# A hybrid decoder block on one core: q and k projected four heads at a time, 512 columns per product, ahead of attention, and kept in DRAM

## The chip, the cores and the metric

The kernel runs on one core of one Trainium2 chip. The metric is the device time in microseconds (us), lower is better. The engines are named as the profile names them: PE is TensorE (matmul), PEld its weight load, DVE is VectorE, ACT is ScalarE, POOL is GpSimd, and SP is SyncE, whose queue issues nearly all DMAs of this kernel. PSUM is the memory that matmuls write; a PSUM bank here holds 128 x 512 numbers of 32 bits.

## The reference

One layer, batch 1, 1024 positions, width 1024, 8 heads. Each head has two queries and two keys of 64 numbers and one value of 128. Cut to what matters here:

```python
h = rms_norm(x, attn_norm_w)
q, k, v, u, g = split(h @ w_in)                  # 1024, 1024, 1024, 2048, 2048 columns
q = rms_norm(q.reshape(B, S, 8, 2, 64), q_norm_w)
k = rms_norm(k.reshape(B, S, 8, 2, 64), k_norm_w)
# per head, causal, with a relative-position bias:
p = softmax(q1 @ k1.T / 8 + bias) - lam * softmax(q2 @ k2.T / 8 + bias)
a = rms_norm(p @ v, subln_w) * (1 - lam_init)
y_a = a @ w_proj_attn
c = silu(layer_norm(causal_depthwise_conv(u_a * sigmoid(u_b))))   # 31 taps
y_b = c @ w_proj_conv
x = x + (sigmoid(g_a) * y_a + sigmoid(g_b) * y_b) @ w_out
x = x + (silu(gate) * up) @ w_down               # gate, up = rms_norm(x) @ w_gate_up
```

## The kernel before

Every product of two matrices is made of three matmuls (`mm3`, lines 152 to 155): each operand is split into a high part and a low remainder, and high x high, high x low and low x high are summed in PSUM. The split of a weight tile is a cast on ACT (line 120) and a subtraction on DVE (line 125).

The work has three stretches. In the first, `h` is made and turned into `hT` (columns in partitions), and then a list of items, `first`, is worked off by generators: `V` (half of v: 512 columns, kept in DRAM), `U` (128 columns of both halves of u for the convolution), `Q` (q and k of one head) and `G` (128 gate columns). At each step of a generator some convolution taps are released as well (`bg`, `TAPS_FIRST` per step): a tap is one DVE instruction over 128 x 1024 (line 610), 31 for each of eight channel blocks, the first of them line 604. The second stretch is attention: 64 steps, one for each head `h` and block `i` of 128 query rows. The third is the projections, the merge and the channel mixer.

An attention step `scores(h, i)` makes both score rows on PE (tile `sc`, three banks), adds the bias and takes the minimum of the negated scores on DVE (line 1153), the exponential and its sum on ACT (line 1158), and combines the two rows on DVE (lines 1164 to 1168). `turn` transposes the result on PE and splits it (ACT, then DVE); `weigh` multiplies it with v for two steps at once; `back` and `subln` finish a head. Between these, `more` puts products of the list `later` that do not depend on attention on PE ("fill"): q and k of the next head (`Q1` to `Q7`), and gates (`G0` to `G13`). The taps that are left are released in attention by `slack`, an estimate of how much longer PE takes for a step than DVE.

A `Q` item (`q_item`, line 790) loads the weights of one head by `ld_wide`: 128 columns of q and 128 of k side by side. `gemm_N` multiplies with `hT` as the stationary and the 256 weight columns as the moving operand; two blocks of 128 rows share one PSUM bank. ACT copies the bank (line 802) into the tile `qkraw` and sums squares for each group of 64 columns (line 805, eight instructions and eight reads of the accumulator a bank). DVE scales 512 rows by the norm (line 812). Later `turn_qk` transposes them on PE (tile `pQ`, line 821), ACT and DVE split them (lines 828 and 830), and DMAs of 128 KB on SP's queue move half rows into place (tiles `qs`, `ks`, `klo`).

The order of instructions on each engine is set when the kernel is built, by a scheduler that places them by its own estimate of times, within what the data and the code's `after(...)` demand; on the chip each engine then runs its own in that order.

Of the kernel before, what the change touches and what calls it, by code (L numbers as in the profile page):

```python
# [57 lines left out]
def kernel(  # L58
# [167 lines left out]
    neglam = cst.tile([P, 1], F32, name="neglam")  # L226
    lsum = cst.tile([P, 2], F32, name="lsum")
# [59 lines left out]
    def wraw():  # L287
        return wp.tile([P, 1024], F32, tag="wraw", name=nm("wraw"), bufs=2)
# [27 lines left out]
    def ld_wide(w, cols):  # L316


        def half(g):
            def go():  # L320
                raw = wraw()
                r3 = raw[:].rearrange("p (k c) -> p k c", c=256)
                o = 0
                for c0, n in cols:
                    nc.sync.dma_start(
                        r3[:, :, o : o + n],
                        w[512 * g : 512 * (g + 1), c0 : c0 + n].rearrange(
                            "(k p) c -> p k c", p=P
                        ),
                    )  # L330
                    o += n
                hi, lo = wsplit(raw)
                return (
                    hi[:].rearrange("p (k c) -> p k c", c=256),
                    lo[:].rearrange("p (k c) -> p k c", c=256),
                )

            return go

        return [half(0), half(1)]  # L340

# [30 lines left out]
    def kt(m, k):  # L372
        return m[k] if isinstance(m, dict) else m[:, k, :]
# [11 lines left out]
    def gemm_N(o, halves, shi, slo, i):  # L385

        ts = slice(i * P, (i + 1) * P)
        for k in range(NKT):
            whi, wlo = halves[k // 4]
            mm3(o, kt(shi, k)[:, ts], kt(slo, k)[:, ts], whi[:, k % 4, :], wlo[:, k % 4, :], k == 0, k == NKT - 1)  # L390


    v_hi = [dr.tile([S, 512], F32, name=f"v_hi{j}") for j in range(2)]
    v_lo = [dr.tile([S, 512], F32, name=f"v_lo{j}") for j in range(2)]
    a_d = [dr.tile([P, S], F32, name=f"a_d{h}") for h in range(H)]
# [15 lines left out]
    first = ["V0", "U0", "U1", "U2", "V1", "U3", "U4", "Q0", "U5", "U6", "U7"]  # L411
    later = [
        ["Q1", "G0", "G1"],
        ["Q2", "G2"],
        ["Q3", "G3"],
        ["G4", "Q4", "G5"],
        ["G6", "Q5"],
        ["Q6", "G7"],
        ["G8", "G9", "Q7"],
        ["G10", "G11", "G12", "G13"],  # L420
        ["G14", "G15"],
    ]
    TAPS_FIRST = 3.25
# [3 lines left out]

    def loads_of(it):
        c = int(it[1:])
        if it[0] == "V":  # L430
            return [ld_pair(win, k, V0 + 512 * c, tiles=vtiles) for k in range(0, NKT, 2)]
        if it[0] == "Q":
            return ld_wide(win, [(Q0 + c * P, P), (K0 + c * P, P)])
# [4 lines left out]
    for it in first[2:] + [x_ for l_ in later for x_ in l_]:  # L438
        ws.plan(loads_of(it))
# [203 lines left out]
    def g_half(c, sb, w, amid=None):  # L643
        o = gemm_T(w, hT_hi, hT_lo, sb, amid)
        sg = wp.tile([P, 512], F32, tag="sg", name=nm("sgg"), bufs=2)
        act.activation(sg[:], o[:], AF.Identity, bias=pcol("gate_b", c))  # L646
        nc.sync.dma_start(g_d[c][:, sb * 512 : (sb + 1) * 512], sg[:])
# [110 lines left out]

    def bias_rows():
# [18 lines left out]
    T = {}  # L778
    late = []

    pools = {}

    def qk_pool():

        if not pools:
            vw_ctx.close()
            pools["qk"] = qk_ctx.enter_context(tc.tile_pool(name="qkp", bufs=2, side="right", reuse_waits="tile"))
        return pools["qk"]

    def q_item(h):  # L790
        qkp = qk_pool()
        halves = [ws.next(), ws.next()]
        t = {}
        T[h] = t
        for b in range(2):
            raw = qkp.tile([P, 4, 256], F32, tag="qkraw", name=nm("qkraw"), bufs=2)
            ss = sm.tile([P, 16], F32, tag="ss16", name=nm("ss16"))
            for i2 in range(2):
                o = pg()
                for e in range(2):  # L800
                    gemm_N(o[:, 256 * e : 256 * (e + 1)], halves, hT_hi, hT_lo, 4 * b + 2 * i2 + e)
                act.copy(raw[:, 2 * i2 : 2 * i2 + 2, :], o[:].rearrange("p (e c) -> p e c", c=256))
                jk = sm.tile([P, VD], F32, tag="jk", name=nm("jk"), bufs=1)[:, :HD]
                for g in range(8):
                    act.activation(  # L805
                        jk, o[:, g * HD : (g + 1) * HD], AF.Square, accum_out=ss[:, 8 * i2 + g : 8 * i2 + g + 1]
                    )
                if i2 == 0:
                    yield
            r = rstd_of(ss[:], 16, 1.0 / HD, fast=h > 0)  # L810
            r4 = raw[:].rearrange("p i (g d) -> p (i g) d", d=HD)
            dve.tensor_tensor(r4, r4, r.unsqueeze(2).to_broadcast([P, 16, HD]), op=ALU.mult)

            def turn_qk(b=b, raw=raw):


                dma = nc.sync.dma_start
                for z, key in enumerate(("q", "k")):
                    pt = pm("pQ")
                    for i in range(4):  # L820
                        pe.transpose(pt[:, i * P : (i + 1) * P], raw[:, i, z * P : (z + 1) * P], ident[:])  # L821
                    w = pcol(key + "n")

                    def part(j):
                        return qkp.tile([P, 512], F32R, tag=f"{key}s{j}", name=f"{key}s{j}_{h}_{b}", bufs=2 if key == "q" else 3)

                    s1, s2 = part(1), part(2)
                    act.activation(s1[:], pt[:], AF.Identity, scale=w)
                    lo = part(3) if key == "q" else qkp.tile([P, 512], F32R, tag="klo", name=f"klo_{h}_{b}", bufs=1)
                    dve.scalar_tensor_tensor(lo[:], pt[:], w, f32(s1[:]), op0=ALU.mult, op1=ALU.subtract)  # L830
                    dma(f32(s2[HD:, :]), f32(s1[HD:, :]))
                    if key == "q":
                        lo2 = part(4)
                        for one, two in ((s1, s2), (lo, lo2)):
                            if one is lo:
                                dma(f32(two[HD:, :]), f32(one[HD:, :]))
                            dma(f32(two[:HD, :]), f32(one[HD:, :]))
                            dma(f32(one[HD:, :]), f32(one[:HD, :]))
                        t["q", b] = (s1, lo), (s2, lo2)
                    else:  # L840
                        dma(f32(s2[:HD, :]), f32(lo[HD:, :]))
                        dma(f32(s1[HD:, :]), f32(lo[:HD, :]))
                        t["k", b] = s1, s2

            late.append((NT * h if b and h else 0, turn_qk))
            yield

    inatt = [False]
    MAKE = {"V": v_item, "U": u_item, "Q": q_item, "G": g_item}

    def run(items):
        for it in items:
            gen = MAKE[it[0]](int(it[1:]))
            while True:
                n = len(late)
                if next(gen, gen) is gen:
                    break
                if not inatt[0]:
                    for _ in range(n):
                        late.pop(0)[1]()  # L860
                yield
# [225 lines left out]
    for _ in chain(opening(), run(first[2:])):  # L1087
# [15 lines left out]
    while late:  # L1103
        late.pop(0)[1]()
# [133 lines left out]
    inatt[0] = True  # L1238
# [3 lines left out]
    fill = run(it for l_ in later[:-1] for it in l_)  # L1242
    plan = [sum(4 if it[0] == "Q" else 2 for it in l_) for l_ in later]
# [15 lines left out]
    def slot(n, nq):  # L1259

        with after(last_fill[0]):
# [5 lines left out]
            for _ in range(nq):  # L1267
                if late[0][0] <= n:
                    late.pop(0)[1]()
# [7 lines left out]
    def slack_of(h, i):  # L1277

        p = (i + 1) * plan[h] // NT - i * plan[h] // NT
        nk = (i + 1) * P  # L1280
        t_pe = nk * (2.52e-3 + (2.5e-3 if i % 2 else 0.0)) + 5.15 * p
        t_dve = 0.4 + 4.2e-3 * nk + p + 0.3
        return max(0.0, t_pe - t_dve)
# [6 lines left out]
    for n, (h, i) in enumerate(steps):  # L1290
        if i == 0:
            load_bias(h)
        p = (i + 1) * plan[h] // NT - i * plan[h] // NT
        nq = len(late)
        scores(h, i)
        scm.append(last_mm[0])
        more((p + 1) // 2)
# [5 lines left out]
        more(p // 2)  # L1303
        slot(n, nq)
# [4 lines left out]
    assert next(fill, None) is None and not late  # L1309
# [61 lines left out]
    inatt[0] = False  # L1371
# [593 lines left out]
```

## Time and profile before

| | |
|---|---|
| median of 3 runs | 1739.37 us (1738.47 to 1739.49) |
| the profiled execution | 1738.13 us, span 1736.3 us |
| granted TensorE clock | 1.00 |
| busy, of the span | PE 1726.8 us, DVE 1292.2, ACT 794.8, POOL 27.1 |
| first score product | 312.3 us after the span's start |
| last score product | 805.8 us |

The page gives for each engine its busy time and, in its groups, line, engine, operation, output and input tiles, count, busy time, the mean duration of one, and idle time before them with what ended it. A "busy" PE does not mean that each matmul takes its recorded duration: the records of consecutive matmuls overlap.

### The profile page before, as it was taken

To read this page: it belongs to the slowest core of one execution; us is meant where nothing else is said; L and a number is where in the kernel's file an instruction comes from. 1 tells how busy PE (TensorE), PEld (TensorE's weight loads), DVE (VectorE), ACT (ScalarE), POOL (GpSimd) and SP (SyncE) were. 2 spreads that over 40 slices of the span, in tenths; PEclk is the share of its full clock that TensorE was granted. 3 is DMA by queue.
4 is the path that set the end of the run, shared out by engine and by line. 5 is a ranking of instruction groups with operands and counts; after the bars stand their busy time and mean duration, and the time that the engine had idled before them with its cause. 6 is when DMAs were issued, how large, how long until landed. Compare 5 with 4: busy or idle time off the path is not lost.

```text
span 1736.3 us, 25111 instructions
## 1 busy us (share of the span) xinstructions
PE 1726.8 (99%) x8954; PEld 1471.5 (85%) x8954; DVE 1292.2 (74%) x2202; ACT 794.8 (46%) x1873; POOL 27.1 (2%) x101
## 2 busy tenths in 40 slices
PE   9999999999999999999999999999999999999999
PEld 6878898999999998988888888888888888888887
DVE  8689988989889898885675567976676666565554
ACT  6121141667767776754564234633333333333332
POOL 0010000000000000000000000000000000000000
PEclk9999999999999999999999999999999999999999
DMA  7269545244444345364874677235445444697663
GB/s 244 91 201 305 183 124 136 71 120 131 122 142 114 89 120 151 87 173 139 288 245 134 200 246 251 86 107 178 152 159 172 158 149 152 224 352 241 218 216 131
DMA packets 260537, 295.22 MB, mean 170 GB/s; under 512 B 17730, under 2 KB 167283, under 8 KB 260412
## 3 DMA queue, kind: packets, MB, share of 16 engines
q1 hardware_dynamic: 257676, 283.73, 50.8%
q0 software_dynamic: 2432, 9.10, 2.2%
q8 instruction: 70, 1.15, 0.3%
q10 hardware_dynamic: 304, 0.79, 0.1%
q14 instruction: 55, 0.45, 0.1%
HBM read 189.19 MB, written 90.21 MB: 161 GB/s over the span
## 4 chain that ended last, share of the span: by engine, by line
PE 95%; DVE 2%; ACT 1%; DMA 1%; issue 0%; SPq 0%; DVEq 0%
PE acc L1819 22%; PE pg L153 14%; PE pg L154 14%; PE pg L155 14%; PE acc L532 12%; PE pg L737 4%; PE wo L1641 3%; PE sc L1152 2%; PE sc L1151 2%; PE pT L1187 2%; PE pW L155 1%; PE pW L153 1%; PE pW L154 1%; PE pQ L821 1%; DMA xa<-in_x_dram 0%; PE tr L1579 0%
## 5 line engine op out<-in xcount | busy, mean ns | idle before, releaser
L610 DVE SCALAR_TENSOR_TENSOR acc<-u,cw,acc 128x1024 f32<-128x1024 f32 x240 | 306.9, 1279 | 2.6
L153 PE MATMUL pg<-hT_hi,whi 128*128 128x512 f32 x512 | 201.5, 394 | 1.2 <-ACT sgg L646 0.9
L154 PE MATMUL pg<-hT_lo,whi 128*128 128x512 f32 x512 | 201.1, 393 | 0.0
L155 PE MATMUL pg<-hT_hi,wlo 128*128 128x512 f32 x512 | 200.8, 392 | 0.0
L120 ACT CAST whi<-wraw 128x1024 fp32r<-128x1024 f32 x101 | 106.3, 1052 | 149.0 <-PE pg L154 96.4
L125 DVE TENSOR_TENSOR wlo<-draw,whi 128x1024 fp32r<-128x1024 f32 x75 | 91.8, 1224 | 89.1 <-ACT whi L120 81.5
L125 DVE TENSOR_TENSOR wlo<-wraw,whi 128x1024 fp32r<-128x1024 f32 x102 | 124.3, 1219 | 44.7 <-ACT whi L120 41.4
L153 PE MATMUL pg<-whi,hT_hi 128*128 128x256 f32 x512 | 146.1, 285 | 0.3 <-ACT jk L805 0.3
L154 PE MATMUL pg<-wlo,hT_hi 128*128 128x256 f32 x512 | 145.7, 285 | 0.0
L155 PE MATMUL pg<-whi,hT_lo 128*128 128x256 f32 x512 | 145.3, 284 | 0.0
L120 ACT CAST whi<-draw 128x1024 fp32r<-128x1024 f32 x75 | 79.1, 1055 | 129.5 <-PE acc L532 119.3
L532 PE MATMUL acc<-wlo,whi 128*128 128x512 f32 x308 | 119.8, 389 | 0.0
L532 PE MATMUL acc<-whi,wlo 128*128 128x512 f32 x308 | 119.8, 389 | 0.0
L153 PEld LDWEIGHTS pg<-hT_hi,whi 128*128 128x128 f32 x512 | 96.2, 188 | 21.3 <-ACT sgg L646 1.7
L154 PEld LDWEIGHTS pg<-hT_lo,whi 128*128 128x128 f32 x512 | 96.2, 188 | 19.4 <-issue 0.6
L155 PEld LDWEIGHTS pg<-hT_hi,wlo 128*128 128x128 f32 x512 | 96.2, 188 | 19.2
L1158 ACT ACTIVATE E<-E,mn 128x256 f32<-128x256 f32 (+7 forms) x128 | 99.4, 778 | 28.2 <-DVE mn L1153 27.9
L153 PEld LDWEIGHTS pg<-whi,hT_hi 128*128 128x128 f32 x512 | 97.6, 191 | 1.9 <-ACT jk L805 0.5
L154 PEld LDWEIGHTS pg<-wlo,hT_hi 128*128 128x128 f32 x512 | 97.6, 191 | 1.5
L155 PEld LDWEIGHTS pg<-whi,hT_lo 128*128 128x128 f32 x512 | 97.6, 191 | 0.7
L1819 PE MATMUL acc<-h_hi,whi 128*128 128x512 f32 x240 | 93.4, 389 | 0.0
L1819 PE MATMUL acc<-h_lo,whi 128*128 128x512 f32 x240 | 93.4, 389 | 0.0
(321 smaller groups left out, 4182.2 us busy)
## 6 DMA issues: line engine op xcount, KB each, us to landing
wraw<-in_w_gate_up_dram SPq DMA_DIRECT2D x44, 512.0 KB, 4.6
wraw<-in_w_in_dram SPq DMA_DIRECT2D x37, 512.0 KB, 5.4
qs<-qs SPq DMA_DIRECT2D x96, 128.0 KB, 2.3
wd<-in_w_down_dram SPq DMA_DIRECT2D x44, 256.0 KB, 3.2
tdT<-wd SPq DMA_DIRECT2D x88, 128.0 KB, 4.2
draw<-sdS SPq DMA_DIRECT2D x44, 256.0 KB
draw<-tdT SPq DMA_DIRECT2D x44, 256.0 KB, 4.3
wraw<-in_w_in_dram SPq DMA_DIRECT2D x32, 256.0 KB, 4.6
```

The lines of the kernel that those rows point to most:

```text
L120: act.copy(dst, src)
L125: last_lo[0] = dve.tensor_tensor(dst, src, f32(hi), op=ALU.subtract).ins
L153: pe.matmul(o, lh, rh, start=start, stop=False)
L154: pe.matmul(o, lh, rl, start=False, stop=False)
L155: last_mm[0] = pe.matmul(o, ll, rh, start=False, stop=stop).ins
L532: m = pe.matmul(o[s_][i][:], l_[:, ts], r_[:, 512:], start=start and j + y_ == 0, stop=j == n - 1 and y_ == 2, skip_group_check=not start,)
L610: dve.scalar_tensor_tensor(acc[0][:], us[c][:, t : t + S], cw[:, c, t : t + 1], acc[0][:], op0=ALU.mult, op1=ALU.add)
L737: last_mm[0] = pe.matmul(o[:], l_, r_, start=first and n_ == 0, stop=last and n_ == len(terms) - 1).ins
L1151: pe.matmul(o[:, :w], qh[:, qs], k, start=True, stop=False)
L1158: act.activation(e[:, :nk], e[:, :nk], AF.Exp, bias=mn[:, j : j + 1], scale=-1.0, accum_out=l[:, j : j + 1])
L1641: last_mm[0] = pe.matmul(o[s_][i][:], l_, r_[:, k, :], start=start and g + k + y_ == 0, stop=g == 1 and k == 1 and y_ == 2, skip_group_che ...
L1819: pe.matmul(o[:], a_[x_][:, k, :], b_[y_][:, k, :], start=start and k + x_ + y_ == 0, stop=k == 3 and x_ == 1, skip_group_check=not start,)
```

## The change

The weights of q and k are no longer taken by head. Items `K0`, `Q0`, `K1`, `Q1` stand in the list `first`; each takes 512 columns (four heads) of k or of q, as the `V` items do, with the same weight tiles (`vwh`, `vwl`, four of each). A row block's bank now holds 128 rows x 512 columns of one of the two; ACT copies it and sums the squares into a table that is kept (`qkss`), and a DMA stores it in DRAM (`qk_d`). In attention, `qk_load` reads 512 rows of one head's q and k back from DRAM into `qkraw`, of which there is now one, `qk_norm` scales it, and `qk_turn` does what `turn_qk` did. `qk_turn` of a head stands three steps ahead of the head for its first half and one step into it for its second, and issues the next load. `later` is gates alone; their generator now yields after half of a 512-column sum, and one such half (12 matmuls) goes into every attention step except the first of a head. The last input item of the convolution, `U7`, stands last in the first stretch, and head 0 is prepared between its steps.

```diff
-    first = ["V0", "U0", "U1", "U2", "V1", "U3", "U4", "Q0", "U5", "U6", "U7"]
-    later = [
-        ["Q1", "G0", "G1"],
...
-        ["G14", "G15"],
-    ]
-    TAPS_FIRST = 3.25
+    first = ["V0", "U0", "U1", "V1", "U2", "K0", "U3", "Q0", "U4", "K1", "U5", "U6", "Q1", "U7"]
+    later = [f"G{c}" for c in range(2 * NKT)]
+    TAPS_FIRST = 3.0
...
     def g_item(c):
         w = ws.next()
         for sb in range(2):
-            g_half(c, sb, w)
+            cs = slice(sb * 512, (sb + 1) * 512)
+            o = pg()
+            for k in range(NKT):
+                mm3(o[:], w[0][:, k, :], w[1][:, k, :], hT_hi[:, k, cs], hT_lo[:, k, cs], k == 0, k == NKT - 1)
+                if k == NKT // 2 - 1:
+                    yield
+            g_out(c, cs, o)
             yield
...
+    def qk_item(z, j):
+        w = [ws.next() for k in range(4)]
+        for i in range(NT):
+            o = pg()
+            v_terms(o, TERMS, w, i, True, True)
+            raw = ap.tile([P, 512], F32, tag=f"v{'hl'[i % 2]}", name=nm("qkr"))
+            act.copy(raw[:], o[:])
+            jk = sm.tile([P, VD], F32, tag="jk", name=nm("jk"), bufs=1)[:, :HD]
+            for g in range(8):
+                act.activation(
+                    jk, o[:, g * HD : (g + 1) * HD], AF.Square, accum_out=qkss[:, i, "QK".index(z), 4 * j + g // 2, g % 2 : g % 2 + 1]
+                )
+            nc.sync.dma_start(qk_d[z][j][i * P : (i + 1) * P, :], raw[:])
+            yield
...
+    def qk_load(h, b):
+
+        raw = pools["qk"].tile([P, 4, 256], F32, tag="qkraw", name=nm("qkraw"), bufs=1)
+        for n_, z in enumerate("QK"):
+            nc.sync.dma_start(
+                raw[:, :, n_ * P : (n_ + 1) * P],
+                qk_d[z][h // 4][b * 512 : (b + 1) * 512, (h % 4) * P : (h % 4 + 1) * P].rearrange("(i p) c -> p i c", p=P),
+            )
+        QR[h, b] = raw
...
+        r4 = raw[:].rearrange("p i (g d) -> p (i g) d", d=HD)
+        dve.tensor_tensor(r4, r4, r.unsqueeze(2).to_broadcast([P, 16, HD]), op=ALU.mult)
...
+        if b == 0:
+            qk_load(h, 1)
+        elif h + 1 < H:
+            qk_load(h + 1, 0)
...
+    turns = {NT * h + d: (h, b) for h in range(H) for b, d in ((0, -3), (1, 1)) if h}
...
-        p = (i + 1) * plan[h] // NT - i * plan[h] // NT
+        p = int(i > 0)
...
-        more((p + 1) // 2)
+        more(int(i > 0))
...
-        slot(n, nq)
+        slot(n)
+        if n + 1 in turns:
+            qk_norm(*turns[n + 1])
```

In the built order, PE before: the last products of an input item of the convolution, then the first of `Q0`, 256 columns wide (the names are those of the tiles, a number telling one buffer from the next).

```order
L154 MATMUL pg_1934<-hT_lo,whi_1693 128x512
L155 MATMUL pg_1934<-hT_hi,wlo_1694 128x512
L153 MATMUL pg_1988<-whi_1832,hT_hi 128x256
L154 MATMUL pg_1988<-wlo_1833,hT_hi 128x256
L155 MATMUL pg_1988<-whi_1832,hT_lo 128x256
```

PE now: the same place in front of the first of the new items, `K0`.

```order
L154 MATMUL pg_1642<-hT_lo,whi_1224 128x512
L155 MATMUL pg_1642<-hT_hi,wlo_1225 128x512
L703 MATMUL pg_1707<-vwh_1528,hT_hi 128x512
L703 MATMUL pg_1707<-vwl_1529,hT_hi 128x512
L703 MATMUL pg_1707<-vwh_1528,hT_lo 128x512
```

1536 products of 256 columns are gone from the program, 768 of 512 are new, and of all of these only the transpositions are left in attention.

DVE in attention before: the scaling of `qkraw` (L812) stands among the splits of weights, the taps (L610) and the score minima (ISA, L1153).

```order
L125 TENSOR_TENSOR wlo_3369<-wraw_3365,whi_3368 128x1024
L610 SCALAR_TENSOR_TENSOR acc_2530<-u_1965,cw,acc_2530 128x1024
L812 TENSOR_TENSOR qkraw_2959<-qkraw_2959,r_3146 128x1024
L1153 ISA E_3275,mn_3263<-sc_3280,tb_2745,mn_3263 128x256
L1153 ISA mn_3263 128x1
L1168 RECIPROCAL rl_0_2761<-l_3264 128x1
```

DVE now, in the last step of head 5: the split of head 6's first half of k (`klo`, L807), and further down the scaling (L787) of its second half, which the loads put into the one `qkraw`; L568 is a tap.

```order
L807 SCALAR_TENSOR_TENSOR klo_0_7256<-pQ_7248,pvec,ks_6_0_7253 128x512
L568 SCALAR_TENSOR_TENSOR acc_5419<-u_3832,cw,acc_5419 128x1024
L1131 ISA E_7364,mn_7352<-sc_7365,tb_6796 128x512
L1131 ISA mn_7352 128x1
L125 TENSOR_TENSOR pl_7217<-pT_7311,ph_7216 128x4x128
L125 TENSOR_TENSOR pl_7217<-pT_7318,ph_7216 128x2x128
L1146 RECIPROCAL rl_5_6812<-l_7353 128x1
L787 TENSOR_TENSOR qkraw_7261<-qkraw_7261,r_7489 128x1024
L1131 ISA E_7364,mn_7352<-sc_7369,tb_6796,mn_7352 128x512
```

The scaling moved from among work that ScalarE had prepared to a place behind a load. In the whole order 112 taps of line 610 stood between the first and the last score minimum; 51 (now line 568) are left there.

SP's queue at the same place now: the two loads of that `qkraw` and the moves of half rows that stand around them.

```order
L814 DMA qs_6_0_7242<-qs_6_0_7239 64x512
L771 DMA qkraw_7261<-Q_d_119 128x4x128
L808 DMA ks_6_0_7254<-ks_6_0_7253 64x512
L815 DMA qs_6_0_7239<-qs_6_0_7239 64x512
L771 DMA qkraw_7261<-K_d_121 128x4x128
L818 DMA ks_6_0_7254<-klo_0_7256 64x512
```

Before, no load of q or k rows stood on this queue; the load of k's part now comes behind a move that needs ACT's split of k.

More of the change, by code (lines that the diff above doesn't have):

```diff
@@ L777 @@
     qk_ctx = ExitStack()
-    T = {}
-    late = []
+    T, QR = {}, {}
     pools = {}
     def qk_pool():
[L785 to L846, printed above, removed]
```

136 lines of the change are left out of this document (67 added, 69 removed).

## The prediction

> **What bounds the kernel now.** I read the page's busy times and chain first, then the busy times of three stretches: up to the first score product (312.3 us), attention (to the last score product, 805.8 us), and the rest.
>
> ```profile
> PE 1726.8 (99%) x8954; PEld 1471.5 (85%) x8954; DVE 1292.2 (74%) x2202; ACT 794.8 (46%) x1873; POOL 27.1 (2%) x101
> ...
> PE 95%; DVE 2%; ACT 1%; DMA 1%; issue 0%; SPq 0%; DVEq 0%
> ```
>
> ```profile
> 0.00:312.30 312.30, 309.55 (x1488) 254.19 (x1489) 262.54 (x310) 86.70 (x180) 11.87 (x32) 1.00 0.57 181
> 312.30:805.80 493.50, 492.17 (x3326) 451.48 (x3325) 435.67 (x1024) 337.25 (x1171) 15.05 (x68) 1.00 0.43 120
> 805.80:1736.30 930.50, 925.06 (x4143) 765.82 (x4142) 593.95 (x869) 370.84 (x522) 0.21 (x1) 1.00 0.58 193
> ```
>
> After the stretch and its length these list PE, weight load, VectorE (DVE), ScalarE (ACT) and POOL busy. TensorE (PE) is the bound everywhere, but in attention VectorE stands at 435.7 of 493.5 us, 88%. So attention's length can fall with its products only until VectorE binds, and that decides this case.
>
> A matmul's record reaches over the start of the next, so prices come from start to start. First a run of 512-column products, then one of 256-column products (start, duration), and the latter's group on the page:
>
> ```profile
> 51.11 0.39 PE L737 MATMUL pg<-vwh,hT_lo 128*128 128x512 f32 x1
> ...
> 61.76 0.39 PE L155 MATMUL pg<-hT_hi,wlo 128*128 128x512 f32 x1
> ```
>
> ```profile
> 218.59 0.28 PE L153 MATMUL pg<-whi,hT_hi 128*128 128x256 f32 x1
> ...
> 228.90 0.28 PE L155 MATMUL pg<-whi,hT_lo 128*128 128x256 f32 x1
> ```
>
> ```profile
> L153 PE MATMUL pg<-whi,hT_hi 128*128 128x256 f32 x512 | 146.1, 285 | 0.3 <-ACT jk L805 0.3
> ```
>
> 47 intervals in 10.65 us are 0.2266 us each; 86 in 10.31 us are 0.1199. The recorded durations (0.39 and 0.285) would promise 1536 x 0.285 - 768 x 0.39 = 138 us from the change; the starts do not.
>
> **PE, step by step.** All heads' q and k take 1536 products of 256 columns before, 768 of 512 after: 1536 x 0.1199 = 184.2 against 768 x 0.2266 = 174.0, a gain of 10.2 us. A sentence on a page: the Trainium skill, "TensorE: Matmul & The Clock Gate", section "Back-to-back issue gap", gives N/2.4 + 2.5 ns between starts, 109.2 and 215.8 ns here, by which widening would gain only 768 x 2.5 ns = 1.9 us, an estimate from that page; the trace shows 119.9 and 226.6, and I use those.
>
> By stretch, from the counts of the two orders. Before the first score there are 785 more 512-column products (1951 against 1166) and no longer 223 of 256: 312.3 + 177.9 - 26.7 = 463.5 us. In attention 1313 of 256 columns (157.4 us), 13 of 512 (2.9 us) and 18 weighted sums (2.2 us, moved behind) go: 493.5 - 162.5 = 331.0 us of PE. The rest is 930.5 + 2.2 - 0.9 = 931.8. With PE as the only bound the span would be 1726.3.
>
> So the first stretch costs 151.2 us more, the rest 1.3 more, and attention has to come down to 493.5 - 152.5 = **341.0 us to break even**.
>
> **VectorE in attention.** Its groups that shrink, and the one that stays:
>
> ```profile
> L610 DVE SCALAR_TENSOR_TENSOR acc<-u,cw,acc 128x1024 f32<-128x1024 f32 x113 | 144.2, 1276 | 0.0
> ...
> L125 DVE TENSOR_TENSOR wlo<-wraw,whi 128x1024 fp32r<-128x1024 f32 x27 | 32.9, 1219 | 2.2 <-ACT whi L120 2.2
> ...
> L812 DVE TENSOR_TENSOR qkraw<-qkraw,r 128x1024 f32<-128x1024 f32 x14 | 17.1, 1221 | 0.1
> ...
> L604 DVE TENSOR_SCALAR acc<-u,cw,pvec 128x1024 f32<-128x1024 f32 x3 | 2.5, 835 | 0.0
> ```
>
> More steps lie ahead of attention (80 against 52, at 3.0 taps instead of 3.25), so in the order 51 convolution taps are left in attention: 113 - 51 = 62 x 1.276 = 79.1 us go, two first taps 1.7, and 14 splits of q and k weights 14 x 1.219 = 17.1 (13 for gates stay). The scaling by the norm stays. That leaves 435.7 - 97.9 = **338 us**, more than PE's 331: VectorE becomes the bound, and its floor is within 3 us of break-even. Everything now hangs on how tightly it can be kept busy.
>
> What it waits for in attention today:
>
> ```profile
> DVE rl L1164 <- ACT E L1158: 14.1, 16, 2.0
> DVE E L1153 <- PE sc L1152: 12.1, 22, 1.7
> DVE rl L1168 <- ACT E L1158: 5.4, 13, 0.9
> DVE E L1153 <- PE pT L1187: 4.2, 6, 1.2
> ```
>
> These are links of one chain: score product, minimum on VectorE, exponential on ScalarE, combination on VectorE, transposition on PE. Its 58 us of waits (493.5 - 435.7) cost nothing while PE binds; once VectorE binds, each counts. How many remain no row shows. Bounds: none (338 us), or all (396 us). The fullest stretches, one ahead of attention (where independent taps fill), one inside:
>
> ```profile
> 160.00:200.00 40.00, 40.00 (x178) 33.11 (x177) 38.24 (x41) 4.96 (x7) 1.33 (x4) 1.00 0.58 194
> ...
> 400.00:440.00 40.00, 40.00 (x280) 37.07 (x280) 36.27 (x82) 26.84 (x78) 1.08 (x6) 1.00 0.39 109
> ```
>
> I take the upper, 38.24/40 = 95.6%, since a saturated engine always has a tap or split queued: 338/0.956 = 353.6 us.
>
> **The new wait: reloading q and k.** Before, the scaling (L812) read what ScalarE had copied from PSUM on the chip. Now the rows come from DRAM into a single buffer (qkraw, one buffer), free only when the preceding transpositions are done; the two loads stand on SP among the half-row moves of q and k, and the scaling (L787) holds VectorE's queue, behind it the score minima that PE waits on through three score banks. For one half head the order has these between the k split (klo) and the scaling: a tap (1.28), a minimum with its read (0.77), two splits (0.69, 0.42), a reciprocal (0.16), about 3 us of work. A load of that size and shape (256 KB in runs of 512 B), and its neighbours on the queue:
>
> ```profile
> qs<-qs SPq DMA_DIRECT2D x96, 128.0 KB, 2.3
> ...
> wraw<-in_w_in_dram SPq DMA_DIRECT2D x32, 256.0 KB, 4.6
> ...
> v_hi<-vh SPq DMA_DIRECT2D x16, 256.0 KB, 3.2
> ```
>
> 4.6 us to landing, issued near klo, leaves 1 to 3 us uncovered there. Over the 14 turns the work in between is 1.8 to 8.9 us, mean 4.6; against 4.5 us needed the shortfalls add up to 10 us, against 6 us (the k load behind more moves) to 22. I take 16. Bounds: 0, and 14 x 4.6 = 64. Attention: 353.6 + 16 = 369.6 us.
>
> **Edits costed at nothing, and their cover.** ScalarE gets the squares of q and k ahead of attention:
>
> ```profile
> L805 ACT ACTIVATE jk<-pg 128x64 f32<-128x64 f32 x224 | 50.7, 226 | 4.3
> L805 ACT ACTIVATION_READ_ACCUMULATOR jk<-pg 128x1 f32 x224 | 45.1, 201 | 0.0
> ...
> L802 ACT COPY qkraw<-pg 128x512 f32<-128x512 f32 x28 | 16.4, 586 | 18.2 <-PE pg L155 18.0
> ```
>
> Per block of rows 8 x 0.427 + 0.586 = 4.0 us, under that block's 24 x 0.2266 = 5.44 us of products; four PSUM banks cover an ACT delay, without them 32 blocks would each expose up to 4 us. Attention's ACT falls by about 110 us. The splits of the next wide weights wait on ScalarE for the previous wide item's last product; a convolution input item (96 products, 21.8 us) covers them, and v's second half does so today. The 32 stores of 256 KB to DRAM have 43.5 us per eight on a queue at 0.57 DMA share. Gate halves keep their products and stores. VectorE ahead of attention: 262.5 + 62 x 1.276 + 1.7 + 17.1 = 360 of 463.5 us.
>
> **The sum.** 463.5 + 369.6 + 931.8 = 1764.9 us of span. The profiled execution took 1738.13 us around its 1736.3; the median of the runs is 1.2 higher. 1764.9 + 1.8 + 1.2 = **1768 us**, 1.6% slower.
>
> **Rivals.**
> - *PE stays the bound.* Attention shrinks to PE's 331 us: 1726.3 + 3 = 1729, faster. For it: VectorE's floor is only 7 us higher, and my removed durations may be off by that; against: in-order VectorE at 100% is nowhere seen. It decides from an attention under 341 us.
> - *VectorE binds without waits.* 463.5 + 338 + 931.8 + 3 = 1736, no change to be told. For it: 51 taps are free to fill gaps; against: the 88% of today.
> - *The chain stays serial.* VectorE keeps its 58 us of waits and adds the 16: 338 + 74 = 412 us, 1810. For it: exponentials and minima alternate within one step; against: much of today's idling only waits for PE.
> - *The clock gate.* The trace's start shows PE at half pace after rest:
>
> ```profile
> 1.19 4.45 PE L929 MATMUL pg<-still 128*128 128x512 bf16 x10 [1.19 <-DVE still L166]
> 5.60 1.06 PE L929 MATMUL pg<-still,mark 128*128 128x512 bf16 x4
> ```
>
> Ten products in 4.45 us, then four in 1.06. If a wait in each head let the clock drop, each return would lose some 2.2 us, eight 18 us: 1786. Against: waits should be 1 to 3 us, with a gate half ahead. The Trainium skill, same page, section "Part 1: The HAM clock gate", says that an idle window of about 3.4 us halves the clock; the start agrees, and no wait in this trace tests it later (granted clock 1.00 throughout).
>
> **How the numbers follow.** Forecast 0.62 (alone 1750 to 1790: reload 0 to 40 us), PE bound 0.10, no waits 0.08, serial 0.13, clock 0.07. A measurement of this kernel tells about 0.2% from no change. Faster 0.10 and the same 0.08 are the first two rivals; slower is the rest, 0.82. A range from 1736 to 1800 leaves out the first rival and most of the serial one.
>
> **What would show it.** Right: first score near 463 us; attention near 370 with VectorE at 90% or more and PE idle some 39 us; the scaling (L787) waiting for qkraw's loads by about 16 us; the rest 932. Wrong: attention at 341 or less, PE without gaps there; a first stretch well over 464, from products waiting for wide weights or PSUM banks; a granted clock under 1.

## The result, and the profile after

The changed kernel takes **1845.82 us** (median of 6 runs, 1842.47 to 1856.15) against 1738.93 of before in the same runs (6 runs, 1738.12 to 1739.49): 1.0621 times, 95% interval 1.0594 to 1.0648. The forecast was 1768, with a range to 1800: the sign was right, the size was not, by 78 us. The profiled execution took 1847.99 us, with a span of 1846.1.

The page of the changed kernel, busy times, the granted clock in 40 slices, and the shares of the chain:

```profile
PE 1765.2 (96%) x8186; PEld 1455.8 (79%) x8186; DVE 1299.9 (70%) x2202; ACT 806.9 (44%) x1875; POOL 27.4 (1%) x101
...
PEclk9999999999989888898899999999999999999999
...
PE 84%; DMA 7%; DVE 5%; issue 2%; ACT 1%; SPq 1%; DVEq 0%; ACTq 0%
```

PE falls from 95% of the chain to 84%; DMAs, 1% before, are 7%, some 130 us. The three stretches (first score product at 463.9 us, last at 910.2), with the columns as before (the 805.8 us of before is the last score minimum; the last score product starts at 805.4, which changes nothing here):

```profile
0.00:463.90 463.90, 460.86 (x2051) 374.73 (x2052) 355.00 (x391) 186.80 (x676) 13.91 (x36) 1.00 0.50 161
463.90:910.20 446.30, 375.55 (x1978) 312.68 (x1978) 346.37 (x934) 247.24 (x672) 12.10 (x61) 0.91 0.44 127
910.20:1846.10 935.90, 928.74 (x4159) 768.42 (x4157) 598.57 (x880) 372.83 (x528) 1.38 (x4) 1.00 0.58 193
```

The forecast had 463.5, 369.6 and 931.8. Two stretches are right within 0.4 and 4.1 us; attention is 76.7 us too long. In it PE is idle for 446.3 - 375.6 = 70.8 us and VectorE for 99.9: neither binds. (PE's 375.6 are more than the 331 us of its products because the granted clock is 0.91 there: at the lower clock a record is longer.)

What PE's score products (tile `sc`) wait for in the changed kernel's attention: idle time in us, times, the longest:

```profile
PE sc L1129 <- DMA qs<-qs: 17.6, 6, 3.8
PE sc L1129 <- DMA ks<-klo: 10.1, 7, 4.1
PE sc L1129 <- DVE mn L1131: 7.4, 10, 1.8
...
PE sc L1130 <- DMA qs<-qs: 3.6, 4, 1.8
```

Three of these four are the half-row moves of q and k, 31.3 us (the weight loads in front of these products stand for much of the same time and are not added). Before, no score product waits for anything. The waits of VectorE in attention show the wait that the prediction was about, and a larger one above it, VectorE's share of the same late scores:

```profile
DVE E L1131 <- PE sc L1130: 28.8, 25, 5.2
DVE rl L1142 <- ACT E L1136: 13.3, 21, 1.3
DVE qkraw L787 <- DMA qkraw<-K_d: 13.2, 8, 3.5
```

One such place, head 1, in the chain that ends attention (start, us, what):

```profile
535.90 0.14 PE pW L155
...
536.06 0.12 ACT ar L1179
...
536.61 0.32 ACT qs L805
...
538.00 0.58 ACT ks L805
...
539.12 0.11 SPq L808
...
539.28 0.59 SPq L814
...
539.96 0.55 SPq L813
...
540.55 5.17 DMA qs<-qs
...
545.79 2.34 DMA qs<-qs
...
548.17 0.79 PE sc L1130
```

ScalarE's split of q (L805) comes behind a copy (`ar`) of the weighted sum on PE; the moves are issued from 538.6 us on, some only when an earlier one has landed (`one` is written over after it has been read twice), and the first score product of the fifth step stands for 3.8 us until moves have landed, a later one (548.17 us) until the last move of this chain has. From the first transposition of the turn (536.0 us) to the first score of the fifth step (546.7) it is 10.7 us; before, the same stretch took 9.1 to 19.2. What differs is what lies under it. Of the second halves' turns of heads 1 to 7 the stretch from the first transposition (tile `pQ`) to the first score of the fifth step, first and last head and the sum of the seven, of before:

```profile
385.30:397.00 11.70, 11.41 (x91) 10.61 (x90) 11.04 (x29) 11.38 (x58) 0.36 (x2) 1.00 0.56 138
...
751.70:770.90 19.20, 19.20 (x107) 16.53 (x106) 16.35 (x45) 10.98 (x35) 0.36 (x2) 1.00 0.64 172
sum 88.00, PE 87.59 PEld 82.04 DVE 74.42 ACT 65.01 POOL 2.65; mean PE 12.51 PEld 11.72 DVE 10.63 ACT 9.29 POOL 0.38
```

and of the changed kernel:

```profile
536.00:546.70 10.70, 4.09 (x23) 2.76 (x21) 9.22 (x28) 5.48 (x21) 0.79 (x4) 0.72 0.88 243
...
879.50:888.70 9.20, 5.89 (x34) 4.55 (x32) 5.48 (x13) 5.21 (x16) 0.36 (x2) 1.00 0.80 224
sum 72.70, PE 38.68 PEld 30.03 DVE 53.71 ACT 41.88 POOL 3.74; mean PE 5.53 PEld 4.29 DVE 7.67 ACT 5.98 POOL 0.53
```

Before, PE has 12.5 us of work under each turn and idles 0.4 us in all seven together. Now it has 5.5 and idles 34.0. The same stretches of the first halves (to the first step of the next head) add up to 95.5 us with 76.4 busy: 19.1 more. So 53 of the 70.8 us of idle PE lie under the turns.

The length of a step by its place in the head, from the starts of the score products, mean over eight heads (us from one step's first score to the next step's; the very last step ends at the last score product):

| step | 1 | 2 | 3 | 4 | 5 | 6 | 7 | 8 |
|---|---|---|---|---|---|---|---|---|
| before | 3.7 | 4.6 | 7.0 | 7.8 | 7.1 | 8.9 | 10.3 | 12.2 |
| after | 3.6 | 5.2 | 4.0 | **14.1** | **10.7** | 3.3 | 5.6 | 9.4 |

Steps 3 and 6 to 8, freed of fill, are now short; the fourth and fifth, where the second half is waited for, are 1.8 and 1.5 times as long.

### The profile page after: what moved, and what is told of

It reads as the page before. It is cut to its first block, busy times and chain, and to the rows that moved or that the text cites. A ratio compares the mean times of both kernels' runs of the same rounds, so it can differ in the third digit from the quotient of the medians.

```text
span 1846.1 us, 23765 instructions
## 1 busy us (share of the span) xinstructions
PE 1765.2 (96%) x8186; PEld 1455.8 (79%) x8186; DVE 1299.9 (70%) x2202; ACT 806.9 (44%) x1875; POOL 27.4 (1%) x101
## 4 chain that ended last, share of the span: by engine, by line
PE 84%; DMA 7%; DVE 5%; issue 2%; ACT 1%; SPq 1%; DVEq 0%; ACTq 0%
PE acc L1794 21%; PE pg L703 13%; PE acc L490 11%; PE pg L153 10%; PE pg L154 10%; PE pg L155 10%; DMA qs<-qs 2%; PE wo L1616 2%; PE sc L1129 1%; PE sc L1130 1%; PE pT L1165 1%; DVE E L1131 1%; DMA ks<-ks 1%; DMA ks<-klo 1%; PE pW L154 1%
## 5 line engine op out<-in xcount | busy, mean ns | idle before, releaser
L568 DVE SCALAR_TENSOR_TENSOR acc<-u,cw,acc 128x1024 f32<-128x1024 f32 x240 | 307.5, 1281 | 4.5
L153 PE MATMUL pg<-hT_hi,whi 128*128 128x512 f32 x512 | 206.4, 403 | 0.2 <-ACT hT_hi L120 0.2
L703 PE MATMUL pg<-vwh,hT_hi 128*128 128x512 f32 x384 | 148.8, 391 | 0.1
L703 PE MATMUL pg<-vwh,hT_lo 128*128 128x512 f32 x384 | 148.5, 390 | 0.0
L703 PE MATMUL pg<-vwl,hT_hi 128*128 128x512 f32 x384 | 147.9, 390 | 0.4 <-DVE vwl L125 0.4
L120 ACT CAST whi<-wraw 128x1024 fp32r<-128x1024 f32 x85 | 89.4, 1051 | 115.7 <-PE pg L154 67.6
L125 DVE TENSOR_TENSOR wlo<-wraw,whi 128x1024 fp32r<-128x1024 f32 x86 | 104.9, 1220 | 46.1 <-ACT whi L120 44.9
L1129 PE MATMUL sc<-ks,qs 128*128 128x512 f32 (+2 forms) x192 | 78.7, 415 | 47.0 <-DMA qs<-qs 17.6
L1131 DVE CUSTOM_DVE_ANT_0 E<-sc,tb 128x512 f32<-128x512 f32 (+3 forms) x128 | 74.2, 587 | 36.3 <-PE sc L1130 24.0
L1794 PE MATMUL acc<-h_hi,wlo 128*128 128x512 f32 x240 | 90.1, 389 | 0.0
```

The costliest lines, as they stand in the source:

```text
L120: act.copy(dst, src)
L125: last_lo[0] = dve.tensor_tensor(dst, src, f32(hi), op=ALU.subtract).ins
L153: pe.matmul(o, lh, rh, start=start, stop=False)
L568: dve.scalar_tensor_tensor(acc[0][:], us[c][:, t : t + S], cw[:, c, t : t + 1], acc[0][:], op0=ALU.mult, op1=ALU.add)
L703: last_mm[0] = pe.matmul(o[:], l_, r_, start=first and n_ == 0, stop=last and n_ == len(terms) - 1).ins
L1129: pe.matmul(o[:, :w], qh[:, qs], k, start=True, stop=False)
```

## The experiments

The theory: with the fill gone the steps became too short for a lead that is counted in steps, and the turns' half-row moves lie open. The rivals: VectorE's load, the clock gate, the reload, and SP's queue held by other work. "The time" is the median of a kernel's runs; attention is measured from the first to the last score product of the profiled execution.

**1. The turns two steps earlier** (e1)

```diff
-    turns = {... for b, d in ((0, -3), (1, 1)) if h}
+    turns = {... for b, d in ((0, -5), (1, -1)) if h}
```

> The turns of q and k stand two steps earlier: five steps ahead of a head for its first half, one step ahead of it for its second (before: three ahead, one into it). Theory 1 (the second half of q and k comes too late: reload, transposition, split and nine half-row moves do not fit into the three short steps before the fifth score step): the step before the fifth score falls from 10 to 18 us to about 6, attention from 446 us to about 375, the granted clock back to 0.99 or more, time about 1775 us. Theory 2 (VectorE is the bound, with 346 us of work and the waits of a serial chain): its work is the same, attention stays within 10 us of 446, time about 1840.

Measured: 1825.36 us, 1.0511 of before (1.049 to 1.0532); attention 421.2 us. The stretches under the second halves' turns are filled, their sum in this run:

```profile
sum 79.00, PE 79.00 PEld 68.57 DVE 60.10 ACT 49.23 POOL 0.07; mean PE 11.29 PEld 9.80 DVE 8.59 ACT 7.03 POOL 0.01
```

The fourth step falls from 14.1 to 6.8 us. But the seventh rises from 5.6 to 12.1, and only 20 us of the 107 are won. Where the turn now stands, the next link shows (chain of this run, head 1):

```profile
544.17 3.43 DMA qs<-qs
...
548.13 2.35 DMA qs<-qs
...
551.06 3.35 DMA qkraw<-K_d
...
554.43 0.04 DVE qkraw L787
```

The next reload stands on SP's queue behind the nine moves, the one buffer allows it no earlier, and the scaling (L787) holds VectorE (17.8 us in eight waits of this run, 13.2 in the changed kernel). Loads of v, 6.6 to 7.7 us each, stand in this run's chain in four heads as well. The time lies between those of the two theories: the place was right, and the next wait took over most of the gain.

**2. No half-row moves** (e2). Left out: the moves, and with them the second arrangement of q and k; the second score row reads the tiles of the first.

```diff
-            dma(f32(s2[HD:, :]), f32(s1[HD:, :]))
...
-                    dma(f32(two[:HD, :]), f32(one[HD:, :]))
-                    dma(f32(one[HD:, :]), f32(one[:HD, :]))
-                t["q", b] = (s1, lo), (s2, lo2)
+                t["q", b] = (s1, lo), (s1, lo)
...
-                t["k", b] = s1, s2
+                t["k", b] = s1, s1
```

> Leaves out the DMAs that move half rows of q and k (both score rows then use the same operand tiles, so the scores are others); everything else stays, the turns at their late places. Theory 1: the moves are most of the lead that is missing, so the long steps shrink and attention falls to about 380 us or less, time about 1780. Theory 2: no VectorE work goes, attention stays near 446, time about 1840.

Measured: 1783.59 us (one run). Its attention:

```profile
465.20:845.80 380.60, 349.56 (x1972) 292.32 (x1970) 335.79 (x925) 246.96 (x674) 11.87 (x61) 0.98 0.32 100
```

The moves are worth 446.3 - 380.6 = 65.7 us of attention. The waits for the reload go with them, since the reload no longer queues behind moves. PE's idle time falls by 39.7 us and its busy time by 26.0, with the granted clock at 0.98 instead of 0.91: a part of the 65.7 may be the slower products that the waits bring with them.

**3. Fewer taps in attention** (e3). Left out: all but two of the 31 taps of a channel block, from attention's start on, 41 VectorE instructions.

```diff
         def tap(t):
             def go():
+                if no_taps and t not in (4, CW - 1):
+                    return
...
+    no_taps.append(1)
     load_v(0)
```

> Leaves out nearly all of the 51 convolution taps that stand in attention (those that issue a DMA stay; the convolution of the last channels is then incomplete): 48 x 1.28 = 61 us less VectorE work there. Theory 2: attention falls by about 55 to 60 us, time about 1788. Theory 1: the long steps wait for DMAs, attention falls by less than 15 us, time above 1830.

Measured: 1824.98 us (one run), attention:

```profile
463.70:890.00 426.30, 371.11 (x1979) 311.42 (x1977) 304.06 (x893) 246.83 (x672) 11.98 (x61) 0.91 0.47 134
```

42 us less VectorE work give 20 us, which neither theory had (under 15, or as much as was taken out). So VectorE's work is a part of what sets the length, and not the whole. VectorE at 71% of attention still leaves it 426 us long: it is not the bound that the forecast took it for.

**4. Products that nobody reads, ahead of the fifth step's scores** (e4). Added: 36 products of 512 columns a head, 8 x 36 x 0.2266 = 65 us of PE work.

```diff
+        if i == NT // 2:
+            with after(scm[-1]):
+                o_ = pg()
+                for e in range(36):
+                    pe.matmul(o_[:], hT_hi[:, e % NKT, :P], hT_hi[:, e % NKT, 512:], start=True, stop=True)
         scores(h, i)
```

> Adds 36 products (8.2 us) whose result nobody reads ahead of the fifth score step of every head, 65 us of TensorE work in all. Theory 1: TensorE idles there anyway, the time stays within 15 us of the changed kernel's 1846. Theory 3 (a good part of the loss is the clock, at half for 85 us of the span, which costs up to 42 us): the idle stretches end, the granted clock goes to 0.99 and the time falls by 20 us or more. If TensorE had no idle time there, the time would grow by 65 us.

Measured: 1847.5 us (one run), attention:

```profile
463.80:911.60 447.80, 411.94 (x2267) 349.17 (x2266) 346.96 (x934) 249.46 (x674) 11.72 (x61) 0.98 0.45 127
```

The granted clock in attention rises from 0.91 to 0.98, 65 us of PE work were added, and attention is 1.5 us longer. PE's idle time falls from 70.8 to 35.9 us: much of the added work lies in time that was waited through. In sum the added work and the higher clock leave the time where it was, but the run doesn't show that the lower clock was free. By the starts of the score products, the fourth and fifth steps are 0.5 and 1.6 us a head shorter than in the changed kernel (13.6 and 9.1 us), and the sixth, behind the added products, is 3.1 longer (6.4). What the clock alone costs was not measured.

**5. Early turns and two buffers for the reload** (e5, the edit of e1 and):

```diff
-        raw = pools["qk"].tile(... tag="qkraw", ..., bufs=1)
+        raw = pools["qk"].tile(... tag="qkraw", ..., bufs=2)
...
-        if b == 0:
-            qk_load(h, 1)
-        elif h + 1 < H:
-            qk_load(h + 1, 0)
+        if h + 1 < H:
+            qk_load(h + 1, b)
...
+        qk_load(0, 1)
...
-            at = aps.tile([P, 512], F32, tag="at", name=nm("at"), bufs=2)
+            at = aps.tile([P, 512], F32, tag="at", name=nm("at"), bufs=1)
```

(`at` gives the room.)

> On top of the earlier turns (1825 us): two buffers for the reloaded rows of q and k, each load issued a whole turn ahead (room for it by one buffer less for the finished head's rows). Theory A (the reload comes late because its single buffer comes free late): VectorE's 18 us of waits for the reload go, with the chain behind them, time about 1800. Theory B (the nine half-row moves ahead of it on SP's queue hold it up): the loads now stand ahead of the moves, so the same 1800. Theory C (what is left are moves and v loads landing late, whatever the reload does): above 1815.

**6. Early turns, the reload on POOL's queue** (e6, the edit of e1 and, in `qk_load`):

```diff
-            nc.sync.dma_start(
+            pool.dma_start(
```

> On top of the earlier turns (1825 us), one buffer: the reloads of q and k are issued from POOL's queue, so that no move on SP's queue stands ahead of them. Theory B: the waits for the reload go, time about 1800. Theory A: the buffer comes free no earlier, the waits stay, time 1815 to 1830.

**7. The edit of e5, the reload and the loads of v on POOL's queue** (e8, `pool.dma_start` in `qk_load` and `load_v`)

> Earlier turns, two buffers for the reload, and both the reloads and the loads of v on POOL's queue, so that SP's queue holds only moves, weights, bias and stores. If the order on SP's queue is what is left (theory B, for v as well: 7 us to landing on the chain in four heads): about 1785. If the moves' own landing times are what is left: within 10 us of the kernel with two buffers.

Measured: e5 1812.46 us, 1.0421 of before (1.0391 to 1.0451), attention 411.7; e6 1817.47, 1.045 (1.042 to 1.048), 415.3; e8 1810.56, 1.041 (1.038 to 1.044), 408.8. The wait of VectorE for the reload is gone in e5, and it gives 9.5 us of attention beside e1; theories A and B had both asked for 1800 us, 12 less than measured. In e6 the waits fall to 8.9 us and do not go, so the single buffer and the queue both have a share. e8 is within 10 us of e5, so the order on SP's queue is not most of what is left. None brings more than 12.4 us of attention beside e1: each takes one link out and leaves the others.

**8. Before, without the moves** (e7; left out as in e2)

> The kernel before, leaving out the DMAs that move half rows of q and k. If the longer steps of its attention (7.7 us in the mean, against 5.6 to 7) hide them, its time stays at 1738 us within 4; the same edit gave the changed kernel 62 us. If they cost there too, it falls by 10 us or more.

Measured: 1736.73 us (one run), against 1739.38 for before in the same runs. The same moves that are worth 62 us in the changed kernel (1845.8 to 1783.6) are worth under 3 in the kernel before: the fill hid them.

**9. The gates twice** (e9). Added: each half of a gate sum is made twice, the second going into a PSUM bank that nobody reads or being written over.

```diff
+                if k % (NKT // 2) == 0:
+                    for e in range(NKT // 2 if k == 0 else 0):
+                        mm3(o[:], w[0][:, e, :], w[1][:, e, :], hT_hi[:, e, cs], hT_lo[:, e, cs], e == 0, e == NKT // 2 - 1)
+                    if k:
+                        d_ = pg()
+                        for e in range(NKT // 2):
+                            mm3(d_[:], w[0][:, e, :], w[1][:, e, :], hT_hi[:, e, cs], hT_lo[:, e, cs], e == 0, e == NKT // 2 - 1)
```

> The changed kernel, with the 12 products of every gate half in attention made twice: the first half's first go is overwritten, the second half's goes into a PSUM bank that nobody reads. That adds 56 x 12 = 672 products of 512 columns, 672 x 0.2266 = 152 us of PE work to attention (331 to 483 us), nothing to any other engine. Theory 1 (the turns' lead is counted in steps, and the steps became too short for the loads and moves; the added work fills the empty steps): attention ends near PE's own sum, 483 to 500 us, so 35 to 55 us more than the 446.3 of the changed kernel and not 152; the waits of scores for qs and ks nearly vanish; the granted clock is 1.00; the time is 1882 to 1902 us. Rival (the waits are a fixed length of time per head, whatever else PE does): attention 446 + 152 = 598 us, the time about 1998 us.

Measured: 1885.49 us (one run). Attention, and the sum of the stretches under the second halves' turns:

```profile
463.50:949.40 485.90, 482.58 (x2645) 412.60 (x2644) 353.70 (x943) 252.39 (x676) 12.56 (x62) 1.00 0.42 118
```

```profile
sum 77.90, PE 77.26 PEld 64.11 DVE 56.22 ACT 46.18 POOL 2.54; mean PE 11.04 PEld 9.16 DVE 8.03 ACT 6.60 POOL 0.36
```

152 us of work cost 39.6. PE is busy for all but 3.3 us, though the turns stand at the same steps of the code as in the changed kernel, and its score products wait for moves 3.3 us instead of 31.3: longer steps alone cover the moves. It also checks the floor: 482.6 - 152.3 is 330.3 us of PE's own work, against 331.0 in the prediction.

**10. Half wide** (e10): heads 0 to 3 as in the change, heads 4 to 7 by head in attention, with the edits of e5 and gates spread over the rest.

```diff
-    first = [... "K0", "U3", "Q0", "U4", "K1", "U5", "U6", "Q1", "U7"]
+    first = [... "K0", "U3", "Q0", "U4", "U5", "U6", "U7"]
+    for n_ in range(H * NT):
+        h_, i_ = n_ // NT, n_ % NT
+        own = {NT * q + d: f"H{q}" for q in range(4, H) for d in (-8, -7, -5, -4)}
+        fills.append([own[n_]] if n_ in own else ["G"] * (2 if h_ not in (3, 4, 5, 6) and i_ in (2, 5) else 1))
...
-        more(int(i > 0))
+        more(fills[n])
```

> A half of the change: q and k of heads 0 to 3 are projected 512 columns wide ahead of attention (K0 and Q0 alone), those of heads 4 to 7 as before by head, 256 columns wide, as fill in attention; gate halves are spread so that nearly every step has one item of fill; the turns lie at five steps and one step ahead of the head's first score (as in the earlier experiment with early turns), qkraw has two buffers. PE's own sum: first score at about 463.5 - 87 = 376.5 us, attention 331 + 4 x 192 x 0.1199 = 423 us, the rest 932. Theory 1 (fill in attention covers the loads, moves and the chain of score, minimum, exponential and combination): with 423 us of PE and about 390 of VectorE attention ends between 425 and 445 us, and the time is 1736 to 1758 us, near the kernel before and 70 us or more under the changed kernel with the early turns and two buffers (1812). Rival (the new path of q and k over DRAM is what costs, whatever the fill): its four heads over DRAM would keep half of that kernel's excess, some 30 to 40 us over PE's sum, and the time is 1765 to 1775 us.

Measured: 1759.83 us, 1.0121 of before (1.0104 to 1.0138). Attention:

```profile
379.90:827.50 447.60, 428.83 (x2732) 380.11 (x2730) 396.12 (x981) 295.03 (x950) 13.59 (x65) 0.99 0.45 128
```

2 us above what the first theory gave and 5 below the rival's: attention is 2.6 us over its upper end, and the first score 3.4 late. 86 us of the excess of 107 are gone, 33 of them with e5's edits alone (1845.8 to 1812.5) and 53 with four heads by head and the fill spread; four heads still go over DRAM, so that path is not by itself what costs. PE idles 18.8 us; its longest wait is for minima (8.4 us at nine scores). It does not beat the kernel before, and no run pointed to a version that would: by the intervals between products all eight heads could gain 10 us of PE, four heads half.

**11. Stores on another queue** (e11)

```diff
-        nc.sync.dma_start(g_d[c][:, cs], sg[:])
+        nc.scalar.dma_start(g_d[c][:, cs], sg[:])
...
-            nc.sync.dma_start(a_d[h][:, sb * 512 : (sb + 1) * 512], at[:])
+            nc.scalar.dma_start(a_d[h][:, sb * 512 : (sb + 1) * 512], at[:])
```

> The changed kernel, with the stores of gates (L604) and of attention's output (L1209) issued on ScalarE's own queue, behind the activation that makes their data, instead of on SP's queue. In the changed kernel's attention the SP queue stood 107.4 us (17 times) at the gate stores and 24.8 us (13 times) at the others, with half-row moves and loads of q, k and v behind them in order. Theory 1 (the second halves are turned too late for their nine moves, counted from the turn itself): the moves wait on one another and on their data, so the long steps stay (about 14 us the fourth of a head, 11 the fifth), attention falls by 15 us at most, and the time is 1831 to 1846 us. Rival (the moves are late because the queue in front of them is held): without the holds the fourth step of a head falls to some 7 us, attention by 40 us or more, and the time is 1805 us or less.

**12. The same on top of e5, with the first move on ScalarE's queue** (e12)

```diff
-            dma(f32(s2[HD:, :]), f32(s1[HD:, :]))
+            nc.scalar.dma_start(f32(s2[HD:, :]), f32(s1[HD:, :]))
```

> The earlier experiment with early turns and two qkraw buffers (1812 us), with the stores of gates and of attention's output and the first half-row move of each operand issued on ScalarE's own queue. There SP stood 70.9 us at the gate stores, 48.2 us at that first move (it waits for ScalarE's activation) and 29.9 us at the other stores. Theory 1 (what is left of the excess there is the chain of scores, minimum, exponential and combination, and the loads of v, none of it a held queue): the time stays within 10 us, 1802 to 1815 us. Rival (the held queue makes the loads of v, 5 to 8 us in the chain, and the moves late): attention falls from 411.7 to about 381, what it was with no moves at all, and the time is 1780 to 1785 us.

Measured: e11 **1856.19** us, 1.0679 (1.0663 to 1.0695), 10 us slower than the change itself, attention 454.1; e12 1803.79, 1.0378 (1.036 to 1.0395), attention 401.3. Taking the 132 us of holds off SP's queue brings the moves no nearer: the fourth and fifth steps of e11 still take 13.2 and 10.5 us, as the first theory had it, and SP now stands at the first move for 65.1 us (31.5 in the changed kernel) and at the loads of v for 52.8 (22.0). That e11 is slower neither theory had, and why was not followed up. In e12 the queue is worth some 9 us, within the first theory's range. The Trainium skill, "Perfetto Trace Analysis", section "DMA Optimizations", suggests one DMA-issuing engine for inputs and another for outputs; here that is 10 us worse in e11 and 9 better in e12, where a half-row move, no output, went along.

Attention's length against PE's own work in it, from these runs:

| | PE work, us (products x 0.2266 or 0.1199) | attention, us |
|---|---|---|
| changed | 331 | 446.3 |
| e4 | 331 + 65 = 396 | 447.8 |
| e10 | 331 + 92 = 423 | 447.6 |
| e9 | 331 + 152 = 483 | 485.9 |
| before | 492 (its busy time) | 493.5 |

With 331 and with 396 us of work attention is equally long; with 483 it is as long as PE's work. (e4 and e9 differ from the changed kernel by the added products alone. e10 has early turns and two buffers as well; with these edits and 331 us of work, e5 has 411.7 us, so 446 is no fixed length either.)

## Why the prediction was wrong

- **The first stretch and the rest**: 463.5 and 931.8 us forecast, 463.9 and 935.9 measured. The intervals of 0.2266 and 0.1199 us, the counts by stretch, and ScalarE's squares and the stores as hidden work all held. The Trainium skill's formula for the interval, which the prediction quotes beside its own, is by its section "Back-to-back issue gap" that of a product by itself and not of a stream; by its 109.2 and 215.8 ns the first stretch would have been 457.4 us, an estimate from that page. Of the 4 us in the rest no cause was sought.
- **PE's floor**: 331.0, checked by e9 at 330.3.
- **VectorE's work**: 338 forecast, 346.4 busy. The durations of VectorE's groups in attention, added up, fall by 99 us (502.7 to 403.4), about as forecast. But busy time counts records that overlap once, and it fell by 89.3. The prediction took recorded durations off a busy time, which it had avoided for PE.
- **"I take the upper, 38.24/40 = 95.6%"**: failed. Without the moves VectorE is at 335.8/380.6 = 88%, just what it was at before, and attention is 27.0 us longer than the 353.6 of this step. The fullest 40 us inside attention of before were not those that the prediction shows, but these, 94.7% full; such a share was reached for a while and not over the whole:

```profile
320.00:360.00 40.00, 40.00 (x254) 36.24 (x254) 37.86 (x77) 24.29 (x91) 0.75 (x4) 1.00 0.32 90
```

  e3 says why the share is no law: less VectorE work did not shorten attention by as much. With neither engine full, the chain of score, minimum, exponential and combination is the likely pace: e2's longest waits are its links (VectorE 18.0 us for exponentials, PE 11.2 for minima). No run isolates it.
- **"The new wait"**: 16 us forecast, 13.2 measured, eight waits of up to 3.5 us. The mechanism was right; it stands behind the moves on SP, as said. That the size came near is in part luck: the loads landed after 3.0 and 3.1 us (median), where the sum had 4.5 to 6, and eight turns of 14 waited.
- **"Edits costed at nothing, and their cover"** has no line on the turns, and this is the step that failed most. The change puts the second half's turn one step later than before, gives its nine moves a lead of a few *steps*, and also empties the steps. The prediction counted the 1313 products that leave attention as time won and didn't ask what they had covered: 10 us a turn, 14 turns. e2 prices it at 65.7 us, with the reload's 13.2 and the slower products in it; e7 shows that the moves cost under 3 us before, and e9 that fill covers them. 353.6 + 27.0 + 65.7 = 446.3, where the 27.0 is what is left over.
- **The rivals**: "the chain stays serial" gave 412 us by another cause (VectorE's 58 us of waits), and attention went past it. The clock gate came, at a granted clock of 0.91 in attention instead of 1.00. What it cost is not told apart: e4 mends most of the clock with 65 us of added work, and the time stays. "PE stays the bound" and "no waits" fell by 105 us and more.
- **Open**: e12 with all its mending stands 21 us over e2, which itself stands 50 over PE's floor. The waits there are many and of 1 to 3 us each; no run took them apart. Nor was the lower clock's own cost measured.

## What to carry to other kernels

A lead that is counted in loop steps is a time only as long as the steps keep their length: where a change takes fill out of a loop, list the transfers and turns that the fill covered, and multiply each one's latency by its count before anything is booked as won. In the built order, add up what an engine has to do between the issue of a transfer and its first reader; where that is 5 us and the latency 10, the rest is a wait. And when no engine is busy nearly throughout a stretch (here PE 84%, VectorE 78%), sums of busy time give a floor but no forecast: here a stretch took 446 to 448 us whether PE had 331 or 396 us of work in it.

## What the runs showed of the hardware

- The granted clock fell to 0.72 in a stretch of 10.7 us in which PE was busy for 4.1, and stayed at 1.00 in attention where PE was busy nearly throughout (e9). Around that stretch the changed kernel's rows (columns as before; the clock is the third number from the end) show when:

```profile
537.30:540.70 3.40, 1.35 (x8) 0.76 (x8) 3.30 (x6) 2.77 (x10) 0.00 (x0) 1.00 1.00 300
540.70:547.50 6.80, 2.29 (x7) 1.43 (x6) 5.02 (x20) 1.48 (x8) 0.42 (x2) 0.50 0.90 234
547.50:554.30 6.80, 6.15 (x23) 5.27 (x23) 4.91 (x11) 2.60 (x5) 0.00 (x0) 0.50 0.27 91
```

  The clock halved after 3.4 us in which PE was busy for 1.35 us and had no gap over 1.6, and it stayed at half for 6.8 us in which PE was busy for 6.15. The Trainium skill, "TensorE: Matmul & The Clock Gate", section "Part 1: The HAM clock gate", has the clock halve after an idle window of about 3.4 us. The half agrees with these rows; that the window has to be idle does not.
- A half-row move of 128 KB landed after 2.3 us (median) before and 3.3 now, singly up to 6.3; the page's rows of before stand in the prediction, and now:

```profile
qs<-qs SPq DMA_DIRECT2D x96, 128.0 KB, 3.3
```

  The stretches under the second halves' turns have the DMA engines 61 to 92% busy, against 45 to 75% before. That alone does not make the moves slow: in e9 the same stretches have 63 to 96%, and the median is 2.4 us. With the early turns, e1, it is 2.3. What makes it 3.3 in the changed kernel stays open.
